# The first norm's shift and scale in three parts, and three tiles of q begun on two feature tiles

## The chip, the cores and the metric

The kernel runs on one core of one Trainium2 chip. A core has five engines that work beside each other, each through its own list of instructions in order: TensorE (PE in the profile, with its weight loads as PEld), VectorE (DVE), ScalarE (ACT), GpSimd (POOL) and SyncE (SP), which here only issues transfers. Transfers between the chip's memory and the core's own memory run on 16 DMA engines that all issuers share. Results of TensorE land in eight PSUM banks, from which DVE and ACT read.

The metric is the time of one execution on the device in microseconds. The three runs shown of the kernel before took 1045.0, 1046.94 and 1053.59 us, median 1046.94. The profile is one more execution, which took 1044.21 us.

## The reference, cut to what matters

One layer of a decoder is computed for 512 prompt tokens and 8 sample tokens, 520 columns in all, with 1024 features. The part that the change touches is its beginning:

```python
sh1, sc1, g1, sh2, sc2, g2 = split(silu(c) @ ada_w + ada_b, 6)     # c: 1 prompt row, 8 sample rows
h = rms_norm(x, norm1_g) * (1.0 + sc1) + sh1
z = h @ w_in        # columns: rg_x | rg_gate | q | k | v | forget | gateA | gateB
# branch A: conv, RG-LRU, gelu gate;  branch B: attention over q, k, v and paged caches
x = x + g1 * ((sigmoid(gA) * A + sigmoid(gB) * B) @ w_o)
x = x + g2 * SwiGLU(rms_norm(x) * (1.0 + sc2) + sh2)
```

All arrays are float32. `ada_w` is 1024 x 6144, so shift and scale of the first norm, its first 2048 columns, are 8.4 MB. The q columns of `w_in` are 1024 x 1024, 4.2 MB.

## The kernel before, in words

**Tiling.** Features lie on the 128 partitions, so x, the normed h and each result are eight feature tiles of 128 x 520. A product is computed in two halves of 260 columns (`HALVES`), one PSUM bank each. The matmuls run in a rounded float32 form; to keep the precision, every weight tile and every activation tile is split into a high part (`hi`, cast by ACT) and a low part (`lo`, the rest, by DVE), and each product of a 128 x 128 weight block is three matmuls: hi x hi, lo x hi, hi x lo (`q_matmuls`, L498 to L504). In the profile they carry the names whi, wlo (weights) and hh, hl (the normed activations).

**The start.** SP issues the loads in the order of the code: parameters, constants, the eight tiles of x, the page table twice (`ptb`, `idx`), then the weights. ACT squares x, DVE adds the squares, TensorE sums them over partitions (L509 to L519). `first_mod(fh, acc, kqs)` loads 128 rows of `ada_w`, 512 columns of the shift and 512 of the scale (512 KB), and multiplies them with silu(c): four narrow matmuls of 256 columns per row block, one for each quarter of the PE columns (profile name adaf). With `fh = 0` all eight row blocks come first. `first_mod_end` then brings the sums back: ACT copies them (adas), TensorE transposes them (adaft), DVE adds the bias (mod) and forms the amplitude (n1amp). That gives shift and scale of feature tiles 0 to 3. Meanwhile DVE computes 1/rms (L525) and scales x (xn, L528).

**h and the first six tiles of q.** `first_h(f)` makes one feature tile of h: ACT the high part of the 512 prompt columns, POOL the 8 sample columns (hr, L476 and L477), ACT their cast (L479), DVE the value (L478) and the low part (L480). The first six 128-column tiles of q are begun with feature tiles 0 to 3 alone, in two groups of three tiles (L538 to L551); the sums so far are kept in `qpart`. Within the first group the eight row blocks of `first_mod(1, ...)` are taken in between, one after every nine matmuls. `first_mod_end(1, ...)` and the h of feature tiles 4 to 7 stand after a quarter of the second group, so 54 matmuls of that group follow them. Later a second part of each q tile (`q_matmuls(1, ...)`) adds feature tiles 4 to 7 and DVE joins both (L878).

**What sets the order.** The code is recorded by a framework that orders each engine's instructions by its own estimates and places the waits; each engine then works strictly in that order. Buffers come from pools: 7 of 4 KB per partition for `ada_w` blocks and cache pages (tag pg), 2 for raw weights (tag wraw, which also holds the forget values of the cache, `past_load`, L405 to L407, gathered by an indirect transfer that POOL issues), 3 each for split weights (whi, wlo), 8 PSUM banks. An instruction that takes a buffer waits until its last reader is done. SP's transfers use eight completion counters in turn, so each transfer waits for the eighth before it.

Of the kernel before, what the change touches and what calls it, by code (L numbers as in the profile page):

```python
# [8 lines left out]
F32 = mybir.dt.float32  # L9
# [12 lines left out]
H = 16  # L22
# [42 lines left out]
def kernel(ctx, tc, xT, par, gates, b_f, cst, cse, own, cache_k, cache_v, cache_lf, pt,  # L65
# [377 lines left out]
    qpart = [slot("qp") for _ in range(6)]  # L443
    amp1 = keep.tile([128, KT, 9], F32, name="n1amp")

    def first_mod(fh, acc, kqs):
        for kq in kqs:
            raw = pgp.tile([128, 2, 512], F32, name="araw", tag="pg")
            sp.dma_start(raw, ada_w[kq * 128:kq * 128 + 128, :2048].rearrange("p (v c) -> p v c", v=2)
                         [:, :, 512 * fh:512 * fh + 512])  # L450
            for g in range(4):
                pe.matmul(acc[32 * g:32 * g + 32, :256], lhsT=silc[:, kq],
                          rhs=raw[:, g // 2, 256 * (g % 2):256 * (g % 2) + 256],
                          start=kq == 0, stop=kq == KT - 1, tile_position=(0, 32 * g))

    def first_mod_end(fh, acc):
        sb = slot("adas", 256)
        act.copy(sb, acc[:, :256])
        tp = bank(f"adaft{fh}")
        for b in range(2):  # L460
            pe.transpose(tp[:, b * 128:b * 128 + 128], sb[:, b * 128:b * 128 + 128], ident)
        tv = tp[:, :256].rearrange("p (b g c) -> p b g c", b=2, g=4)
        fs = slice(4 * fh, 4 * fh + 4)
        for v in (1, 0):
            dve.tensor_tensor(
                mod[:, v, fs].rearrange("p (q b) c -> p b q c", b=2), tv[:, :, 2 * v:2 * v + 2, 0:9],
                prm[:, fs, P_AB + v:P_AB + v + 1].rearrange("p (q b) c -> p b q c", b=2).to_broadcast([128, 2, 2, 9]),
                ALU.add)
        dve.scalar_tensor_tensor(amp1[:, fs], mod[:, 1, fs], 1.0, prm[:, fs, P_N1:P_N1 + 1].to_broadcast([128, 4, 9]),
                                 ALU.add, ALU.mult)  # L470

    def first_h(f):
        t, hi, lo = slot("hr"), slot("hh", dt=F32R), slot("hl", dt=F32R)
# [8 lines left out]

    xn = []

    def q_weights(fh, raw, ko, i):
# [5 lines left out]
        for k in range(0, 4, 2 if (fh, i) == (0, 0) else 4):  # L491
            ks = slice(k, k + 2 if (fh, i) == (0, 0) else 4)
            state["act"] = act.copy(hi[:, ks], src[:, ks])
            state["last"] = dve.tensor_tensor(lo[:, ks], src[:, ks], hi[:, ks].bitcast(F32), ALU.subtract)
# [15 lines left out]
    for f in range(KT):  # L510
# [9 lines left out]
    acc = [bank(f"adaf{fh}") for fh in range(2)]  # L520
    first_mod(0, acc[0], range(KT))
    r1 = slot("r1")
    for j, (t0, t1) in enumerate(HALVES):
        act.activation(r1[:, t0:t1], ssq[j][:, :HALF], AF.Sqrt, bias=eps, scale=1.0 / D)
        dve.reciprocal(r1[:, t0:t1], r1[:, t0:t1])  # L525
    for f in range(KT):
        t = slot("xn")
        dve.tensor_tensor(t, x[f], r1, ALU.mult)  # L528
        xn.append(t)
    raw = wraw()  # L530
    q_weights(0, raw, 0, 0)
    first_mod_end(0, acc[0])
    for f in range(4):
        first_h(f)
    q_weights(0, raw, 4, 2)
    raw = wraw()
    q_weights(0, raw, 0, 4)
    for g3 in (0, 3):  # L538
        banks = [bank(f"qp{i}_{j}") for i in range(g3, g3 + 3) for j in range(2)]
        for k in range(4):  # L540
            for n in range(6):
                q_matmuls(0, g3 + n // 2, n % 2, k, banks[n])
                if g3 == 0 and n % 3 == 2:
                    first_mod(1, acc[1], (2 * k + n // 3,))
            if g3 and k == 0:
                first_mod_end(1, acc[1])
                for f in range(4, KT):
                    first_h(f)
        for n in range(6):
            t0, t1 = HALVES[n % 2]  # L550
            act.copy(qpart[g3 + n // 2][:, t0:t1], banks[n][:, :HALF])  # L551
        if g3 == 0:
            flr = slot("flr", KT * H).rearrange("p (k c) -> p k c", k=KT)
            sp.dma_start(flr, w_in[:, COL_FL:COL_FL + H].rearrange("(k p) c -> p k c", p=128))
    raw = wraw()
    q_weights(1, raw, 0, 0)
    q_weights(1, raw, 4, 2)
# [1149 lines left out]
```

## Time and profile before

| | us |
|---|---|
| median of three runs (1045.0 to 1053.59) | 1046.94 |
| the profiled execution | 1044.21 |
| its span in the profile | 1042.3 |
| PE busy | 998.9 (96% of the span) |
| DVE busy | 777.5 (75%) |
| ACT busy | 533.2 (51%) |
| POOL busy | 304.0 (29%) |
| moved by DMA | 206.97 MB, mean 199 GB/s |

The span is the time from the first to the last recorded instruction; 1.9 us of the execution lie around it. The 40 slices of the page are 26 us each. A row of the timeline is: start in us, duration in us, engine, line of the kernel, operation, tile written <- tiles read, sizes, how many merged into the row, and in brackets how long the engine had been idle before and what ended it. A row of a table of stretches is: stretch, its length, then for each engine its busy time and count, then the granted TensorE clock (1.00 is full), the DMA share and GB/s.

### The profile page before, as it was taken

To read this page: it belongs to the slowest core of one execution; us is meant where nothing else is said; L and a number is where in the kernel's file an instruction comes from. 1 tells how busy PE (TensorE), PEld (TensorE's weight loads), DVE (VectorE), ACT (ScalarE), POOL (GpSimd) and SP (SyncE) were. 2 spreads that over 40 slices of the span, in tenths; PEclk is the share of its full clock that TensorE was granted. 3 is DMA by queue.
4 is the path that set the end of the run, shared out by engine and by line. 5 is a ranking of instruction groups with operands and counts; after the bars stand their busy time and mean duration, and the time that the engine had idled before them with its cause. 6 is when DMAs were issued, how large, how long until landed. Compare 5 with 4: busy or idle time off the path is not lost.

```text
span 1042.3 us, 21246 instructions
## 1 busy us (share of the span) xinstructions
PE 998.9 (96%) x8054; PEld 925.8 (89%) x8054; DVE 777.5 (75%) x1370; ACT 533.2 (51%) x1072; POOL 304.0 (29%) x411
## 2 busy tenths in 40 slices
PE   4999999999999999999999999899999999999993
PEld 1888899999898988878888989899999999999993
DVE  5447999988989978886665546778589558869663
ACT  4523665857671467767793234555244324524451
POOL 0224411112133235654500003472224033223113
PEclk9999999999999999999999999999999999999997
DMA  9898987787889999996766863132343234143212
GB/s 326 295 306 289 300 281 216 262 253 270 263 253 309 321 326 284 303 274 213 263 230 209 282 226 82 41 82 75 100 111 83 91 111 121 54 128 102 75 52 83
DMA packets 165353, 206.97 MB, mean 199 GB/s; under 512 B 9842, under 2 KB 126082, under 8 KB 165186
## 3 DMA queue, kind: packets, MB, share of 16 engines
q1 hardware_dynamic: 148530, 152.52, 47.2%
q0 software_dynamic: 13040, 46.67, 13.5%
q10 hardware_dynamic: 3680, 6.42, 1.7%
q8 instruction: 63, 1.03, 0.4%
q14 instruction: 40, 0.33, 0.1%
HBM read 192.49 MB, written 13.09 MB: 197 GB/s over the span
## 4 chain that ended last, share of the span: by engine, by line
PE 70%; DVE 12%; DMA 7%; ACT 5%; issue 4%; POOL 1%; SPq 0%; POOLq 0%; DVEq 0%; ACTq 0%
PE fo L281 11%; PE fi_S L1578 7%; PE fi_A L1578 5%; PE pb L281 4%; PE gb L281 4%; PE fig L281 4%; PE fiu L281 4%; PE ga L281 3%; PE k L281 3%; PE wo L281 3%; PE v L281 3%; DVE wlo L228 2%; PE gr L281 2%; PE xr L281 2%; DMA wraw<-in_w_in_dram 2%
## 5 line engine op out<-in xcount | busy, mean ns | idle before, releaser
L226 ACT CAST whi<-wraw 128x1024 fp32r<-128x1024 f32 (+2 forms) x113 | 111.4, 987 | 186.1 <-PE fo L281 45.0
L228 DVE TENSOR_TENSOR wlo<-wraw,whi 128x1024 fp32r<-128x1024 f32 (+2 forms) x113 | 137.3, 1216 | 48.6 <-ACT whi L226 40.9
L281 PE MATMUL fo<-ach,whi 128*128 128x260 f32 x302 | 85.6, 283 | 0.0
L281 PE MATMUL fo<-ach,wlo 128*128 128x260 f32 x302 | 85.2, 282 | 0.0
L281 PE MATMUL fo<-acl,whi 128*128 128x260 f32 x302 | 85.0, 282 | 0.0
L658 POOL DMA_DIRECT2D pg<-in_cache_k_dram x74 | 39.4, 533 | 142.4 <-DVE S L707 70.5
L241 POOL TENSOR_TENSOR ws<-wraw 128x512 f32<-128x512 f32 x13 | 20.0, 1538 | 193.5 <-DMA wraw<-in_w_fi_dram 188.7
L706 DVE TENSOR_TENSOR pg<-pg,qb 128x1024 f32<-128x1024 f32 x48 | 58.0, 1227 | 2.4 <-DMA pg<-in_cache_k_dram 2.4
L707 DVE TENSOR_REDUCE S<-pg 128x16 f32<-128x1024 f32 x48 | 57.0, 1207 | 0.1
L281 PEld LDWEIGHTS fo<-ach,whi 128*128 128x128 f32 x302 | 56.8, 188 | 0.2
L281 PEld LDWEIGHTS fo<-ach,wlo 128*128 128x128 f32 x302 | 56.8, 188 | 0.0
L281 PEld LDWEIGHTS fo<-acl,whi 128*128 128x128 f32 x302 | 56.8, 188 | 0.0
L1191 POOL TENSOR_SCALAR p<-p,mu 128x128 f32<-128x128 f32 (+3 forms) x28 | 35.9, 1293 | 48.2 <-DVE mu L1187 31.6
L249 DVE TENSOR_TENSOR wb<-ws,wb 128x512 fp32r<-128x512 f32 x52 | 45.8, 891 | 4.2 <-ACT wb L248 4.1
L373 POOL TENSOR_TENSOR ss<-ss,sq 128x260 f32<-128x260 f32 x18 | 13.7, 761 | 111.3 <-PE ada L344 58.9
L248 ACT CAST wb<-ws 128x512 fp32r<-128x512 f32 x52 | 31.5, 619 | 26.2 <-PE fi_S L1578 8.6
L1185 ACT ACTIVATE p<-p,mu 128x128 f32<-128x128 f32 (+3 forms) x64 | 35.3, 552 | 15.8 <-DVE mu L1184 15.5
L248 ACT CAST wb<-wraw 128x512 fp32r<-128x512 f32 x39 | 23.9, 620 | 34.7 <-PE fo L281 18.1
L1396 DVE SCALAR_TENSOR_TENSOR x<-fo,mod,x 128x252 f32<-128x252 f32 x32 | 15.2, 477 | 32.4 <-PE fo L281 32.4
L1435 ACT CAST ach<-sw 128x260 fp32r<-128x260 f32 (+1 forms) x42 | 17.6, 419 | 41.5 <-DVE sw L1477 22.3
L281 PE MATMUL v<-hh,whi 128*128 128x260 f32 x128 | 37.3, 291 | 1.1 <-DVE pl L1205 1.1
L1578 PE MATMUL fi_S<-twh,wb 128*128 128x260 f32 x208 | 38.1, 282 | 0.0
(435 smaller groups left out, 4065.7 us busy)
## 6 DMA issues: line engine op xcount, KB each, us to landing
araw<-in_ada_w_dram SPq DMA_DIRECT2D x48, 512.0 KB, 6.2
wraw<-in_w_fi_dram SPq DMA_DIRECT2D x44, 512.0 KB, 5.2
pg<-in_cache_k_dram POOLq DMA_DIRECT2D x42, 512.0 KB, 6.2
pg<-in_cache_v_dram SPq DMA_DIRECT2D x42, 512.0 KB, 5.5
wraw<-in_w_in_dram SPq DMA_DIRECT2D x34, 512.0 KB, 7.7
wraw<-in_w_in_dram SPq DMA_DIRECT2D x11, 1024.0 KB, 10.3
pg<-in_cache_v_dram POOLq DMA_DIRECT2D x22, 512.0 KB, 6.4
pg<-in_cache_k_dram POOLq DMA_DIRECT2D x32, 256.0 KB, 5.7
```

The costliest lines, as they stand in the source:

```text
L226: state["act"] = act.copy(hi[:, :k1 - k0], src)
L228: state["last"] = dve.tensor_tensor(lo[:, :k1 - k0], src, hi[:, :k1 - k0].bitcast(F32), ALU.subtract)
L241: pool.tensor_tensor(s1, a21, a22, ALU.add)
L248: state["act"] = act.copy(t[:, :4], src)
L249: state["last"] = dve.tensor_tensor(t[:, 4:], src, t[:, :4].bitcast(F32), ALU.subtract)
L281: state["mm"] = pe.matmul(out[:, :HALF], lhsT=wt[k], rhs=at, start=k == 0 and m == 0, stop=k == nk - 1 and m == 2)
L658: done.append(eng.dma_start(pg, cache[bass.ds(r, 1), :, c0:c1].rearrange("a p c -> (a p) c")))
L706: dve.tensor_tensor(pg, pg, q, ALU.mult)
L707: last = dve.tensor_reduce(S[r // 2][:, c:c + H], pg.rearrange("p (h d) -> p h d", d=DH), AX.X, ALU.add)
L1185: act.activation(p[:, :n + 128], p[:, :n + 128], AF.Exp, bias=mu[:, 0:1], scale=-1.0, accum_out=mu[:, 1:2])
L1191: (pool.tensor_scalar(p, p, mu[:, 2:3], None, ALU.mult) if a and i + 1 < KT else act.activation(p, p, AF.Copy, scale=mu[:, 2:3]))
L1578: state["mm"] = pe.matmul(b, lhsT=wt[k], rhs=at, start=k == 0 and m == 0, stop=k == 3 and m == 2)
```

## The change

`ada_w`'s columns for the first norm come in three parts. Features 0 to 255 and 256 to 511 are "quarters": 256 columns of shift and 256 of scale, eight loads of 256 KB each, matmuls of 128 columns (`quarter_load`, `quarter_mod`). Features 512 to 1023 come as before, eight loads of 512 KB (`first_mod`). `first_mod_end` takes the first feature tile and a count, and forms the amplitude ahead of the shift. The loads of the page table move from the start to behind the second quarter.

The weights of q for the first half of the features come in four parts of 256 rows by 384 columns (`q_part`), not three of 512 rows by 256 columns. After the first quarter, feature tiles 0 and 1 of h are made in halves, in place of xn (`early_h`), and q tiles 0 to 2 begin with them; the second quarter's matmuls lie between these. Then feature tiles 2 and 3 follow, then q tiles 3 to 5 with all four tiles, the third part's matmuls between them, and only then `first_mod_end(4, 2, ...)` and h of feature tiles 4 to 7.

```diff
-    sp.dma_start(ptb, pt.rearrange("a b -> (a b)")[None, :])
-    sp.dma_start(idx, pt.rearrange("a (b c) -> (a b) c", c=1))
...
+    def quarter_load(q, kq):
+        if kq % 2 == 0:
+            quarters[q, kq // 2] = pgp.tile([128, 2, 2, 256], F32, name="qraw", tag="pg")
+        sp.dma_start(quarters[q, kq // 2][:, kq % 2],
+                     ada_w[kq * 128:kq * 128 + 128, :2048].rearrange("p (v c) -> p v c", v=2)
+                     [:, :, 256 * q:256 * q + 256])
+
+    def quarter_mod(q, acc, kqs):
+        for kq in kqs:
+            raw = quarters[q, kq // 2][:, kq % 2]
+            for g in range(4):
+                pe.matmul(acc[32 * g:32 * g + 32, :128], lhsT=silc[:, kq],
+                          rhs=raw[:, g // 2, 128 * (g % 2):128 * (g % 2) + 128],
+                          start=kq == 0, stop=kq == KT - 1, tile_position=(0, 32 * g))
...
+    def early_h():
+        for f in range(2):
+            h.append((slot("hh", dt=F32R), slot("hl", dt=F32R)))
+        for j, (t0, t1) in enumerate(HALVES):
+            e_ = min(t1, NP)
+            for f in range(2):
+                t, (hi, lo) = xn[f], h[f]
+                a_, b_ = amp1[:, f, 0:1], mod[:, 0, f, 0:1]
+                act.activation(hi[:, t0:e_], t[:, t0:e_], AF.Identity, scale=a_, bias=b_)
+                if j:
+                    pool.tensor_tensor(t[:, NP:], t[:, NP:], amp1[:, f, 1:9], ALU.mult)
+                    pool.tensor_tensor(t[:, NP:], t[:, NP:], mod[:, 0, f, 1:9], ALU.add)
+                    act.copy(hi[:, NP:], t[:, NP:])
+                dve.tensor_scalar(t[:, t0:e_], t[:, t0:e_], a_, b_, ALU.mult, ALU.add)
+                dve.tensor_tensor(lo[:, t0:t1], t[:, t0:t1], hi[:, t0:t1].bitcast(F32), ALU.subtract)
...
+    def q_part(raw, k0, i, step):
+        src = raw[:, k0:k0 + 2]
+        sp.dma_start(src, w_in[128 * k0:128 * k0 + 256, COL_Q + 128 * i:COL_Q + 128 * i + 384]
+                     .rearrange("(k p) c -> p k c", p=128))
...
-    first_mod(0, acc[0], range(KT))
+    for kq in range(6):
+        quarter_load(0, kq)
+    q_part(raw, 0, 0, 1)
+    for kq in range(6, KT):
+        quarter_load(0, kq)
+    quarter_mod(0, accs[0], range(KT))
+    for kq in range(KT):
+        quarter_load(1, kq)
     r1 = slot("r1")
+    xn.extend(slot("xn") for _ in range(KT))
     for j, (t0, t1) in enumerate(HALVES):
         act.activation(r1[:, t0:t1], ssq[j][:, :HALF], AF.Sqrt, bias=eps, scale=1.0 / D)
         dve.reciprocal(r1[:, t0:t1], r1[:, t0:t1])
...
+        for f in range(2):
+            dve.tensor_tensor(xn[f][:, t0:t1], x[f][:, t0:t1], r1[:, t0:t1], ALU.mult)
+    first_mod_end(0, 1, accs[0])
+    early_h()
+    for f in range(2, KT):
+        dve.tensor_tensor(xn[f], x[f], r1, ALU.mult)
+    q_part(raw, 2, 0, 2)
+    sp.dma_start(ptb, pt.rearrange("a b -> (a b)")[None, :])
+    sp.dma_start(idx, pt.rearrange("a (b c) -> (a b) c", c=1))
...
+    for (j, k), kqs in zip(((0, 0), (0, 1), (1, 0), (1, 1)), ((0, 1, 2), (3,), (4, 5), (6, 7))):
+        for i in range(3):
+            q_matmuls(0, i, j, k, banks[i, j])
+        quarter_mod(1, accs[1], kqs)
+    first_mod_end(2, 1, accs[1])
+    first_h(2)
+    first_h(3)
+    q_part(raw, 0, 3, 2)
+    q_part(raw, 2, 3, 2)
+    acc = bank("adaf2")
+    for k in (2, 3):
+        for j in range(2):
+            for i in range(3):
+                q_matmuls(0, i, j, k, banks[i, j])
...
+    for k in range(4):
+        for j in range(2):
+            for i in range(3, 6):
+                q_matmuls(0, i, j, k, banks[i, j])
+            if k < 3 or j == 0:
+                first_mod(acc, ((0, 1), (2,), (3,), (4,), (5,), (6,), (7,))[2 * k + j])
+    first_mod_end(4, 2, acc)
+    for f in range(4, KT):
         first_h(f)
```

More of the change, by code (lines that the diff above doesn't have):

```diff
@@ L464, in first_mod_end @@
         for v in (1, 0):
[L465 to L470, printed above, removed]
+            bias = prm[:, fs, P_AB + v:P_AB + v + 1]
@@ L483 @@
     xn = []
+    def q_part(raw, k0, i, step):
+        src = raw[:, k0:k0 + 2]
+        sp.dma_start(src, w_in[128 * k0:128 * k0 + 256, COL_Q + 128 * i:COL_Q + 128 * i + 384]
+                     .rearrange("(k p) c -> p k c", p=128))
+        hi = wp.tile([128, 2, 384], F32R, name="whi", tag="whi", bufs=3)
+        lo = wp.tile([128, 2, 384], F32R, name="wlo", tag="wlo", bufs=3)
+        for k in range(0, 2, step):
+            ks = slice(k, k + step)
+            state["act"] = act.copy(hi[:, ks], src[:, ks])
+            state["last"] = dve.tensor_tensor(lo[:, ks], src[:, ks], hi[:, ks].bitcast(F32), ALU.subtract)
+        for n in range(3):
+            cs_ = slice(128 * n, 128 * n + 128)
+            qw.setdefault((0, i + n), []).extend((hi[:, k, cs_], lo[:, k, cs_]) for k in range(2))
     def q_weights(fh, raw, ko, i):
@@ L490, in q_weights @@
         src = raw[:, ko:ko + 4]
[L491 to L494, printed above, removed]
+        state["act"] = act.copy(hi, src)
+        state["last"] = dve.tensor_tensor(lo, src, hi.bitcast(F32), ALU.subtract)
         for n in range(2):
```

69 lines of the change are left out of this document (31 added, 38 removed).

## The prediction

> **What bounds the kernel now.** I read the page first (span, busy shares), then a table of stretches, then the timeline of the first 60 us, then the order and waits of the changed kernel as built.
>
> ```profile
> span 1042.3 us, 21246 instructions
> PE   4999999999999999999999999899999999999993
> ```
> ```profile
> 20.00:25.43 5.43, 1.97 (x18) 0.60 (x18) 4.49 (x10) 2.23 (x4) 0.95 (x2) 0.78 1.08 356
> 25.43:29.10 3.67, 3.67 (x15) 3.43 (x15) 3.56 (x7) 3.48 (x6) 3.48 (x6) 0.50 1.05 384
> ...
> 51.40:58.00 6.60, 6.60 (x58) 6.58 (x57) 4.33 (x7) 2.30 (x6) 1.59 (x3) 1.00 0.61 193
> ...
> 100.00:110.00 10.00, 9.36 (x78) 9.13 (x77) 10.00 (x20) 4.75 (x10) 7.49 (x15) 1.00 1.03 353
> 110.00:120.00 10.00, 9.23 (x74) 8.81 (x73) 9.79 (x25) 5.35 (x10) 4.66 (x10) 1.00 0.77 230
> ```
>
> TensorE is busy in every slice but the first and the last, so a microsecond that it loses or wins early moves the end, unless a later wait of its own takes it up. Up to 25.43 it starves: the first product of q begins then, and from there it runs without a pause. The change works on this start and on what follows up to about 59 us.
>
> ```profile
> 1.79 4.04 SPq L99 DMA_DIRECT2D x<-in_xT_dram  x8
> ...
> 9.04 2.67 ACT L512 ACTIVATE sq<-x 128x520 f32<-128x520 f32 x4 [0.48 <-DMA x<-in_xT_dram]
> ...
> 14.53 3.41 DVE L525 RECIPROCAL r<-r 128x260 f32<-128x260 f32 x2 [1.84 <-ACT r L524]
> ...
> 17.98 4.97 DVE L528 TENSOR_TENSOR xn<-x,r 128x520 f32<-128x520 f32 x8
> ...
> 22.04 0.64 PE L452 MATMUL adaf<-araw,silc 128*32 128x256 f32 x8 [0.73 <-DMA araw<-in_ada_w_dram]
> ...
> 23.17 0.69 PE L461 MATMUL adaft<-cs,adas 128*128 128x128 f32 x2 [0.49 <-ACT adas L458]
> 23.52 1.14 ACT L493 CAST whi<-wraw 128x512 fp32r<-128x512 f32 x2 [0.41 <-DMA wraw<-in_w_in_dram]
> 23.89 0.29 DVE L465 TENSOR_TENSOR mod<-adaft,prm 128x36 f32<-128x36 f32 x2 [0.94 <-PE adaft L461]
> ...
> 24.24 1.29 DVE L494 TENSOR_TENSOR wlo<-wraw,whi 128x512 fp32r<-128x512 f32 x2
> ...
> 24.57 0.81 ACT L475 ACTIVATE hh<-xn,mod,n1amp 128x512 fp32r<-128x512 f32 x1
> ...
> 25.43 0.58 PE L503 MATMUL qp<-hh,whi 128*128 128x260 f32 x1 [1.57 <-ACT hh L475]
> ```
> ```profile
> 18.00:21.00 3.00, 1.58 (x24) 0.43 (x24) 3.00 (x5) 0.00 (x0) 0.00 (x0) 1.00 1.04 383
> 22.00:25.00 3.00, 1.33 (x10) 0.45 (x10) 2.06 (x7) 1.85 (x4) 0.58 (x1) 0.68 1.09 349
> ```
>
> The last square begins at 9.04 + 3 x 0.67 = 11.0, so x has landed by then. The eight 512 KB blocks (4.19 MB) take until 22.04, 381 GB/s, and 3.4 us pass from the last block to the first product: copy, transposes, shift and scale, h. DMA is full the whole time.
>
> **Step 1, the start: -3.4 us.** Before the first product now stand eight quarters (2.10 MB) and 0.39 MB of weights. Their runs of 1 KB arrive as the weights of q do in the stretch 22 to 25, at 349 GB/s, not at the 383 of the 2 KB runs. The weights stand seventh: 1.97 MB, landed at 11.0 + 5.6 = 16.65. The last quarter: 18.15. Now DVE's list decides. Behind the first reciprocal (1.7, to 16.2) stand the two low parts of the weights, which wait for ACT's casts of 384 (0.43 each): 17.15 to 18.15. Then two half xn (0.31 each), to 18.75; the second reciprocal, to 20.45; the scale (0.15), 20.6; two half xn, 21.2; amplitude and shift, 21.5. ACT's half hh (0.45) ends at 21.95, TensorE starts at 22.05. The transfers alone would have let it start a good half microsecond to one earlier. Bounds: the weights at 383 GB/s land 0.5 earlier (-3.9); landing 2 later gives -1.4. The Trainium skill (DMA: Bandwidth & Descriptors, Specifications) gives 512 B as the least transfer for line rate, by which 1 KB runs would cost nothing against 2 KB; the trace differs with 349 against 383 GB/s. By that rule of the Trainium skill step 1 would be -3.9.
>
> **Step 2, work that moves onto TensorE's path: +3.1 us.** In the kernel before, the first eight groups of adaf ran while TensorE starved, the other eight inside q. Now eight quarter groups run while it starves, and eight quarter groups and eight full ones inside q.
>
> ```profile
> 33.29 0.64 PE L452 MATMUL adaf<-araw,silc 128*32 128x256 f32 x8
> ...
> 34.80 0.28 PE L503 MATMUL qp<-hl,whi 128*128 128x260 f32 x1
> 34.92 0.28 PE L503 MATMUL qp<-hh,whi 128*128 128x260 f32 x1
> 35.14 0.64 PE L452 MATMUL adaf<-araw,silc 128*32 128x256 f32 x8
> ```
> ```profile
> 60.18 1.06 PE L344 MATMUL ada<-araw,silc 128*32 128x512 f32 x8
> ```
>
> A group and nine products take 35.14 - 33.29 = 1.85; products follow each other at 0.12, so a group costs 1.85 - 9 x 0.12 = 0.77. One of 512 columns lasts 1.06 against 0.64: 0.42 per 256 columns, so 0.21 for 128 and 0.35 for changing over. As built, the second quarter is entered five times: 8 x 0.21 + 5 x 0.35 = 3.4. The third part is entered seven times: 8 x 0.42 + 7 x 0.35 = 5.8 for the 8 x 0.77 = 6.2 of before. One transpose more is 0.1. Bounds: columns free, 1.4; each quarter group as dear as a full one, 5.8. The 144 products stay, and I leave the 15 slow ones at the start (clock 0.50) as they are.
>
> **Step 3, behind the second quarter: +0.8 us.** The transpose of feature tiles 2 and 3 stands right behind the quarter's last group on TensorE and waits for ACT's copy, which stands behind a weight cast that waits for a buffer freed by the products just before. That is 0.5. Eleven products of q tiles 3 and 4 (1.3 us) then cover most of the way to hh; 0.3 is left. Bounds: 0, and 2.6, the time from 22.04 + 0.64 = 22.68 to 25.43 of before, less the one transpose that is saved.
>
> **Step 4, before the second half of the features: +4.3 us.** In the kernel before, this is hidden: shift and scale of tiles 4 to 7 come with 54 products still to do.
>
> ```profile
> 44.52 0.38 PE L461 MATMUL adaft<-cs,adas 128*128 128x128 f32 x2
> ...
> 51.24 0.28 PE L503 MATMUL q<-hh,whi 128*128 128x260 f32 x1
> ...
> 54.23 0.28 PE L503 MATMUL q<-hh,wlo 128*128 128x260 f32 x1
> ```
> ```profile
> 45.28 1.22 DVE L494 TENSOR_TENSOR wlo<-wraw,whi 128x1024 fp32r<-128x1024 f32 x1
> 46.41 0.54 DVE L478 TENSOR_SCALAR hr<-xn,n1amp,mod 128x512 f32<-128x512 f32 x1
> 47.27 0.73 DVE L480 TENSOR_TENSOR hl<-hr,hh 128x520 fp32r<-128x520 f32 x1 [0.32 <-ACT hh L479]
> ...
> 51.09 0.70 DVE L480 TENSOR_TENSOR hl<-hr,hh 128x520 fp32r<-128x520 f32 x1
> ```
> ```profile
> 45.40 0.82 ACT L475 ACTIVATE hh<-xn,mod,n1amp 128x512 fp32r<-128x512 f32 x1 [0.86 <-DVE n1amp L469]
> ...
> 50.03 1.05 ACT L493 CAST whi<-wraw 128x1024 fp32r<-128x1024 f32 x1 [0.38 <-ACT hh L479]
> ```
> ```profile
> 55.26 1.20 POOL L407 DMA_INDIRECT lfp<-in_cache_lf_dram,idx  x1 [5.93 <-DVE wlo L494]
> ```
>
> Now only nine products stand between the third part's last group and the two transposes. Call their end E. From transpose to amplitude pass 0.88 (44.52 to 45.40). On ACT a cast of 1.05 is queued ahead of the first hh, and its buffer comes free at E: hh of tile 4 runs from E + 1.1 to E + 1.9. On DVE follow the value of tile 4 (0.54, to E + 1.4), the low part of those weights (1.13 to the next), to E + 2.5, and four low parts with their values, 47.27 to 51.79 in the kernel before, 4.5: E + 7.0. The built order puts 25 products before the first one that needs the last low part, 54.23 - 51.24 = 3.0, and the transposes are 0.25: 3.8 of standing still. POOL adds 0.5: the gather lfp stands in its list before the shift of tile 5's sample columns, and its buffer waits for that same weight low part at E + 2.5; with 1.20 for itself and 0.4 for the shift the samples come at E + 4.1, ACT's cast is queued behind them, and DVE's low part of tile 5, else due at E + 3.8, at E + 4.3. Bounds: 3.3 (each low part 0.1 faster, no POOL delay) to 5.8.
>
> **Step 5, afterwards: -0.7 us.** TensorE's order is the same from there on. Of its 0.64 + 0.77 of waits from 100 to 120, when DVE is full, I take off half: one `ada_w` block and one gate block will have been loaded ahead of where TensorE is, so pages come a little earlier to DVE. Moving the page table costs nothing: POOL reads it between h of tiles 0 and 1 (to about 23) and that of tiles 2 and 3 (from 33); landing after 33, it would hold up that h by as much. SP issues nine transfers more, half a microsecond each (4.04 for eight of x); with eight in flight, over 2 MB, the full DMA covers them, and were it to run dry each would cost its 0.5 on step 1.
>
> **Sum:** -3.4 + 3.1 + 0.8 + 4.3 - 0.7 = +4.1, on the profiled 1044.2: 1048.3. The median of the runs lies 2.7 above the profiled execution, the lowest run 0.8; I add 1.2 and forecast **1049.5**, 0.4% slower. That is no change by what a measurement of this kernel can tell, about 1%. Its own range is 1047 to 1052.
>
> **Rival, faster: the delay is taken up later.**
>
> ```profile
> 200.00:300.00 100.00, 98.16 (x804) 90.95 (x803) 90.58 (x114) 70.19 (x124) 17.93 (x34) 1.00 0.80 256
> 300.00:400.00 100.00, 97.20 (x778) 88.34 (x780) 89.71 (x142) 46.35 (x99) 38.14 (x57) 1.00 1.00 306
> 400.00:500.00 100.00, 98.30 (x745) 83.09 (x738) 79.33 (x172) 74.49 (x187) 52.24 (x77) 1.00 0.87 263
> ```
>
> TensorE waits 1.8 + 2.8 + 1.7 = 6.3 here and 1.4 before. If these waits hang on the stream of cache pages through a full DMA to a 90% busy DVE, and that stream starts no later, all 7.7 can go: 4.8 - 7.7 = -2.9, 1042.5. It decides once more than 4.8 of them go. For it speaks the full DMA, against it that DVE and ACT are fed by TensorE's own results too. Chance 0.15.
>
> **Rival, the clock falls again.** The mean of 0.68 from 22 to 25 is 1.00 for 1.1 us and 0.50 after, so it fell at 23.1, although TensorE had been busy 1.58 of 3 us from 18 to 21. In step 4 it is busy 3.2 of 7.0. At 0.50 the 15 products from 25.43 took 3.67 in place of 1.8; as long a spell adds 2 to 3.4: 1051.5 to 1053. Chance 0.2. The Trainium skill (TensorE: Matmul & The Clock Gate, What's actually happening) lets it fall after an idle window of some 3.4 us; no pause here reaches 2 us, so by that rule the clock would hold and nothing be added; the trace speaks against it, since it fell at 23.1 without such a pause.
>
> **Rival, the change doesn't start q earlier:** quarters and weights land so late that the first product stays near 25.4. Then step 1 is nothing and the time 1053. DMA that is full speaks against it; chance 0.07.
>
> **How the numbers follow.** Forecast 0.5, the rivals 0.15, 0.2 and 0.07, unlisted slips 0.08. The range is 1042.5 to 1056: down to the faster rival, up to the clock's fall with step 2 at its upper bound (+2.7). Faster by over 1% (10.5 us) needs more than step 1 and all waits together: 0.02. Slower by over 1% needs the clock, a late start and an upper bound at once: 0.07. Within: 0.91.
>
> **What would show it.** The first product near 22; between 22 and 32 adaf records in five bunches; an idle TensorE of 3 to 5 us in two or three pieces near 52 to 59, waited for ACT hh and DVE hl; POOL's lfp in the middle of the hr rows; the clock after 52; the 26th product of the second half near 59, not 54.23. The prediction is wrong if that idle time is under 2, if the quarter groups cost under 0.25 each, or if the waits from 100 to 500 shrink by more than 3.

## The result and the profile after

| | kernel before | changed kernel |
|---|---|---|
| median | 1047.24 us (8 runs, 1045.0 to 1053.59) | 1054.97 us (8 runs, 1051.01 to 1058.55) |
| profiled execution, span | 1044.21, 1042.3 | 1056.78, 1055.1 |
| first product of q | 25.43 | 22.01 |
| first ada group | 60.18 | 66.24 |

The changed kernel takes 1.0058 times as long (95% interval 1.0031 to 1.0085, that is 3.2 to 8.9 us). The medians differ by 7.7 us, the two profiled spans by 12.8. By the bound of 1% that is no change; by the interval it is slower.

The slices of the changed kernel's page: TensorE is as full as before.

```profile
PE   4999999999999999999999999999999999999993
```

The timeline of the changed kernel, in the order of the prediction's steps:

```profile
22.01 0.39 PE L549 MATMUL qp<-hh,whi 128*128 128x260 f32 x1 [2.94 <-ACT hh L498]
...
32.05 0.33 PE L475 MATMUL adaft<-cs,adas 128*128 128x128 f32 x1 [0.56 <-ACT adas L472]
...
51.62 0.38 PE L475 MATMUL adaft<-cs,adas 128*128 128x128 f32 x2
53.64 0.39 PE L549 MATMUL q<-hh,whi 128*128 128x260 f32 x1 [1.63 <-ACT hh L509]
...
54.86 0.39 PE L549 MATMUL q<-hl,whi 128*128 128x260 f32 x1 [0.47 <-DVE hl L514]
...
56.40 0.49 PE L549 MATMUL q<-hh,whi 128*128 128x260 f32 x1 [0.80 <-ACT hh L513]
...
66.24 1.06 PE L344 MATMUL ada<-araw,silc 128*32 128x512 f32 x8
```
```profile
54.49 1.38 POOL L405 DMA_INDIRECT lfp<-in_cache_lf_dram,idx  x1 [0.24 <-DVE wlo L540]
55.90 0.22 POOL L511 TENSOR_TENSOR hr<-hr,mod 128x8 f32<-128x8 f32 x1
```
```profile
56.38 0.73 DVE L514 TENSOR_TENSOR hl<-hr,hh 128x520 fp32r<-128x520 f32 x1 [1.12 <-ACT hh L513]
...
58.93 0.70 DVE L514 TENSOR_TENSOR hl<-hr,hh 128x520 fp32r<-128x520 f32 x1
```

q starts 3.4 earlier, and at 51.62 the third part ends. From there TensorE stands still three times (1.63, 0.47, 0.80), and the first ada group, which stands at the same place in TensorE's list in both kernels, comes 66.24 - 60.18 = 6.06 later. From that point on TensorE's two lists are the same, so the lag can be read at any later product: 5.85 at 100 us of the kernel before, 7.31 at 130, 7.2 at 280, 8.8 at 300, 12.9 at 390, 12.8 at 1000. The lists of the other engines are not the same: the framework ordered them anew.

The table of stretches of the changed kernel shows what came on top of the 6.06:

```profile
53.11:56.52 3.41, 1.61 (x9) 1.20 (x10) 2.29 (x4) 1.65 (x5) 3.06 (x6) 1.00 1.05 406
56.52:59.94 3.42, 3.37 (x15) 3.07 (x16) 2.91 (x5) 3.09 (x10) 1.03 (x3) 0.50 1.11 374
105.00:130.00 25.00, 22.62 (x180) 21.57 (x179) 20.48 (x50) 11.85 (x24) 10.49 (x22) 1.00 0.86 274
285.22:288.63 3.41, 1.54 (x16) 1.05 (x9) 3.41 (x5) 3.38 (x7) 1.58 (x3) 1.00 0.43 115
288.63:292.04 3.41, 3.41 (x18) 3.41 (x17) 3.41 (x6) 2.04 (x7) 1.06 (x2) 0.50 1.02 345
391.03:394.44 3.41, 1.76 (x9) 1.29 (x10) 3.38 (x6) 2.94 (x6) 0.00 (x0) 1.00 1.03 393
394.44:397.86 3.42, 3.42 (x17) 3.42 (x18) 2.25 (x11) 1.96 (x9) 0.00 (x0) 0.50 1.05 331
```

TensorE waits 25 - 22.62 = 2.4 us between 105 and 130; over the same products, from 99 to 124, it had waited 1.4. And three times the granted clock is 0.50 for 3.41 us, called a half clock from here on: at 56.52, 288.63 and 394.44. At 288.63 the kernel before has the same wait of the same length, and no half clock:

```profile
280.34 0.51 PE L955 MATMUL gate<-xch,gws 128*128 128x260 f32 x2 [1.84 <-ACT gate L956]
```
```profile
275.66:279.08 3.42, 2.85 (x24) 1.79 (x22) 3.42 (x5) 2.35 (x4) 0.28 (x1) 1.00 0.60 169
279.08:282.49 3.41, 2.15 (x17) 2.15 (x18) 3.41 (x5) 3.40 (x9) 1.83 (x4) 1.00 0.68 240
```

All starts of a half clock in one execution lie whole multiples of 3.413 us apart. In the changed kernel the 1.87 us of that wait fell into one such interval (busy 1.54 of 3.41), in the kernel before it was cut by a boundary (2.85 and 2.15).

Of the 6.8 us that the lag grows behind the ada group, 1.2 come by 130 us, 1.5 with the half clock at 288.63, and 4.1 between 300 and 390. They come with the half clock at 394.44 and, ahead of it, with waits for DVE and ACT that sum to 2.3 us, where the first profile of the kernel before has 0.75 and its second (c0 below) 2.0.

### The profile page after: what moved, and what is told of

It is laid out like the page before. It is cut to its first block, busy times and chain, and to the rows that moved or that the text cites. A ratio compares the mean times of both kernels' runs of the same rounds, so it can differ in the third digit from the quotient of the medians.

```text
span 1055.1 us, 21395 instructions
## 1 busy us (share of the span) xinstructions
PE 1007.3 (95%) x8118; PEld 933.1 (88%) x8118; DVE 780.7 (74%) x1380; ACT 533.6 (51%) x1076; POOL 299.9 (28%) x411
## 4 chain that ended last, share of the span: by engine, by line
PE 75%; DVE 12%; DMA 4%; ACT 4%; issue 2%; POOL 1%; SPq 0%; POOLq 0%; ACTq 0%; DVEq 0%
PE fo L281 11%; PE fi_S L1647 7%; PE fi_A L1647 5%; PE pb L281 4%; PE gb L281 4%; PE fiu L281 4%; PE v L281 4%; PE fig L281 4%; PE k L281 4%; PE pa L281 3%; PE wo L281 3%; PE ga L281 3%; PE gr L281 2%; PE pv L860 2%; DMA wraw<-in_w_in_dram 2%
## 5 line engine op out<-in xcount | busy, mean ns | idle before, releaser
L241 POOL TENSOR_TENSOR ws<-wraw 128x512 f32<-128x512 f32 x13 | 17.5, 1345 | 194.5 <-DMA wraw<-in_w_fi_dram 186.5
L1647 PE MATMUL fi_A<-h2h,wb 128*128 128x260 f32 x208 | 38.2, 284 | 0.0
```

The source lines that it names most:

```text
L1647: state["mm"] = pe.matmul(b, lhsT=wt[k], rhs=at, start=k == 0 and m == 0, stop=k == 3 and m == 2)
```

## Experiments: what holds TensorE between 51 and 66 us

**The third part earlier (e1_cover).** Four of the eight row blocks go into the first group of q tiles, so that some 40 products follow the last block, not 9.

```diff
     for k in (2, 3):
         for j in range(2):
             ...
+            first_mod(acc, (2 * k + j - 4,))
...
-            if k < 3 or j == 0:
-                first_mod(acc, ((0, 1), (2,), (3,), (4,), (5,), (6,), (7,))[2 * k + j])
-    first_mod_end(4, 2, acc)
-    for f in range(4, KT):
-        first_h(f)
+            if 2 * k + j < 3:
+                first_mod(acc, ((4, 5), (6,), (7,))[2 * k + j])
+            if 2 * k + j == 2:
+                first_mod_end(4, 2, acc)
+                for f in range(4, KT):
+                    first_h(f)
```

> The changed kernel with the third part's groups begun ten products earlier: four row blocks inside the first group of q tiles, four in the second, so that about 40 products stand behind the last block in place of 9. Theory (the chain from the third part's last block to the last low part of tile 7, 8.0 us in the changed kernel, stands open): 40 products of 0.12 and the 25 that need no last low part cover 7.8 of 8.0; TensorE's waits for hh and hl before the second half of the features fall from 2.9 us to under 0.7, no half clock near 57, the first ada group stands near 60.8 and not at 66.24, and the median falls by 5 us, to about 1050. Rival 1 (the third part's loads are late, because its eighth block waits for the buffer of its first): TensorE waits for araw instead, 2 us or more, and the time is 1053 or above. Rival 2 (what is won early is lost again at 100 to 500): the ada group near 61, but the median above 1053.

Measured: 1054.76 us (1.0064, 1.004 to 1.0089), the ada group at 65.98. The theory fell, and so did both rivals: TensorE didn't wait for araw, and nothing was won at the ada group that could be lost later. ACT's, POOL's and TensorE's timelines of this run say why:

```profile
53.25 1.05 ACT L539 CAST whi<-wraw 128x1024 fp32r<-128x1024 f32 x1 [1.57 <-issue]
...
57.52 0.20 ACT L513 CAST hh<-hr 128x8 fp32r<-128x8 f32 x1 [1.70 <-POOL hr L511]
```
```profile
55.87 1.37 POOL L405 DMA_INDIRECT lfp<-in_cache_lf_dram,idx  x1 [2.26 <-DVE wlo L540]
```
```profile
48.10 0.42 PE L475 MATMUL adaft<-cs,adas 128*128 128x128 f32 x2
...
57.77 0.39 PE L549 MATMUL q<-hh,whi 128*128 128x260 f32 x1 [0.79 <-ACT hh L513]
```

The transposes came 3.5 earlier, and the h of tiles 6 and 7 didn't follow: ACT's third weight cast stood 1.57 us, with hh of those tiles queued behind it, and POOL's gather waited for the low part of those weights, with the samples of tile 7 behind it.

**The two queues cleared (e9_queue).** The same, with POOL's gather put behind the samples of tile 7 (`hr` is POOL's last instruction for them) and the third weight cast behind ACT's last hh:

```diff
-            past_load()
+            with tc.issue_after(state["hr"].ins):
+                past_load()
...
-    q_weights(1, raw, 0, 4)
+    with tc.issue_after(state["hh"].ins):
+        q_weights(1, raw, 0, 4)
```

> The run with the earlier third part, and beside it two queues cleared: POOL's gather lfp behind the samples of tile 7, and ACT's third weight cast (with its low part on DVE) behind the last hh; that cast had stood 1.57 us at 53.25 for a buffer, with hh of tiles 6 and 7 behind it. Theory (the end of the third part was covered, but the h of tiles 4 to 7 stood behind a cast that waits for the last products of the first half, and behind the gather): TensorE's waits at 54 to 58 (0.47, 0.41, 0.79) all go, no half clock near 58, the first ada group 0.4 to 1.0 us later than the 60.18 of the kernel before, and few waits at 100 to 130: median 1048 to 1049.5. Rival (the casts and the gather only swap places with other waits, for the weights' low part held back): the group above 63 and the median above 1052.

Measured: the waits of 0.47, 0.41 and 0.79 are gone but for 0.29, the clock holds there, and the ada group stands at 62.00, 4.2 earlier than in the changed kernel (0.8 later than expected). So the two queues together were what held it; this run doesn't say what each is worth. The median, 1053.48 (1.0061, 1.0039 to 1.0082), missed the expectation by 4; the section on what becomes of a delay takes that up.

**The gather alone (e2_gather)** has the first hunk of that diff and nothing else.

> The changed kernel with POOL's gather lfp held back until the sample columns of tile 7 are shifted. Theory (the gather holds up tile 5's samples and so the whole row of low parts): the shift of tile 5 ends near 54.5 and not 56.12, the wait of 0.80 for hh ahead of tile 5 is gone, tile 7's low part ends near 58.7 and not 59.63, and the first ada group stands 0.5 to 0.9 earlier than 66.24: median 1054.3. Rival (the half clock from 56.5 on sets the pace there, not the low parts): the group stands less than 0.3 earlier where the clock has fallen, and more than 1.2 earlier where it has not.

Measured: 1053.36 us (1.0066, 1.0041 to 1.0091), and in the timeline and the stretches:

```profile
52.02 0.38 PE L475 MATMUL adaft<-cs,adas 128*128 128x128 f32 x2
...
57.78 0.38 PE L549 MATMUL q<-hl,whi 128*128 128x260 f32 x1 [0.28 <-DVE hl L514]
...
65.09 1.06 PE L344 MATMUL ada<-araw,silc 128*32 128x512 f32 x8
```
```profile
58.29 0.70 DVE L514 TENSOR_TENSOR hl<-hr,hh 128x520 fp32r<-128x520 f32 x1
```
```profile
53.57:56.98 3.41, 2.19 (x13) 1.78 (x14) 3.25 (x5) 2.56 (x7) 3.25 (x5) 1.00 1.05 409
56.98:60.40 3.42, 3.14 (x25) 2.81 (x24) 2.62 (x5) 2.35 (x8) 2.03 (x4) 1.00 0.28 89
```

Counted from the transposes, the last low part ends after 6.97 us in place of 8.01, and the ada group comes after 13.07 in place of 14.62. Of those 1.55, the earlier low parts are 1.0. The other 0.5 is put down to the half clock, which this run doesn't have there: the 26th product of the second half starts at 59.04, 0.05 behind the last low part, and in the changed kernel at 60.30, 0.67 behind it. That price is low because the low parts set the end of this stretch in any case. The group stands 1.15 earlier than 66.24, more than the theory's 0.5 to 0.9 and just under the rival's 1.2; low parts and clock each have a share.

**The wait filled (e3_fill)**: 13 products behind the transposes (`tp` is the last of them), into a bank that is free.

```diff
     first_mod_end(4, 2, acc)
+    with tc.issue_after(state["tp"].ins):
+        for n in range(13):
+            pe.matmul(acc[:, :HALF], lhsT=h[0][0][:, :128], rhs=h[0][0][:, :HALF], start=True, stop=True)
```

> The changed kernel with 13 more products, whose result nobody reads, behind the transposes of the third part, in the wait of 1.63 us for hh of tile 4: TensorE is busy there. Theory (the clock falls after an interval of 3.4 us in which TensorE is busy less than half, and the last low part at 59.63 sets the end of this stage in any case): no half clock between 50 and 62, and still the first ada group only 0.5 us earlier, near 65.7; median lower by 0.5, 1054.5. Rival (the price that the prediction set, 2 to 3.4 us for the clock): the group near 63 to 64 and the median near 1052.

```profile
53.50:56.91 3.41, 2.05 (x13) 1.44 (x11) 2.29 (x4) 1.66 (x5) 3.06 (x6) 1.00 1.06 408
56.91:60.33 3.42, 3.26 (x15) 2.95 (x15) 2.79 (x5) 2.96 (x10) 0.90 (x2) 0.50 1.09 366
```

Measured: 1053.53 us (1.0068, 1.0043 to 1.0094), the ada group at 66.57, 14.68 behind the transposes as in the changed kernel (14.62). The first wait was filled, and the clock fell all the same. Theory and rival both had the group earlier, and it isn't. The run says little about the first wait, though: in this execution the interval ahead of the fall begins at 53.50, when the filled wait was nearly over. The two later waits were enough, with TensorE recorded busy for 2.05 of 3.41.

## Experiments: what the start is worth

**The second reciprocal later (e5_recip; `amp` is the first amplitude), the page table at the start again (e4_tables), the second quarter in one bunch (e6_bunch).**

```diff
-        dve.reciprocal(r1[:, t0:t1], r1[:, t0:t1])
+    for j, (t0, t1) in enumerate(HALVES):
+        with tc.issue_after(state["amp"].ins) if j else nullcontext():
+            dve.reciprocal(r1[:, t0:t1], r1[:, t0:t1])
         for f in range(2):
             ...
-    first_mod_end(0, 1, accs[0])
+        if j == 0:
+            first_mod_end(0, 1, accs[0])
```
```diff
     ptb = keep.tile([1, NS * NPAGE], I32, name="ptb")
     idx = keep.tile([NS * NPAGE, 1], I32, name="idx")
+    sp.dma_start(ptb, pt.rearrange("a b -> (a b)")[None, :])
+    sp.dma_start(idx, pt.rearrange("a (b c) -> (a b) c", c=1))
...
     q_part(raw, 2, 0, 2)
-    sp.dma_start(ptb, pt.rearrange("a b -> (a b)")[None, :])
-    sp.dma_start(idx, pt.rearrange("a (b c) -> (a b) c", c=1))
```
```diff
-    for (j, k), kqs in zip(((0, 0), (0, 1), (1, 0), (1, 1)), ((0, 1, 2), (3,), (4, 5), (6, 7))):
+    for (j, k), kqs in zip(((0, 0), (0, 1), (1, 0), (1, 1)), ((), (), (), range(KT))):
```

> The changed kernel with DVE's second reciprocal behind the first amplitude. Theory (step 1: DVE's list, not the transfers, decides when q starts): the first product at 20.3 to 21.0 in place of 22.01. Rival (the last quarter's landing decides): 21.8 or later. At 51.6, where the third part ends, the theory leaves 0.3 to 1.0 of it, since the second halves come later by the same reciprocal; the median falls by that much, below what the runs can tell.

> The changed kernel with the two loads of the page table at the start again, behind x. Theory (their move costs and brings nothing, since DMA is full there): the first product of q within 0.3 of 22.01, the first ada group within 0.4 of 66.24, the median within 2 of 1055. Rival (two issues of 0.5 us on SP ahead of all weights count): the first product 0.6 to 1.0 later, and the median about 1056.

> The changed kernel with all eight groups of the second quarter in one bunch behind the first 36 products, not in five. Theory (step 2: each change between products and groups costs 0.35 us): four changes less, the third part's transposes at 50.2 to 50.6 in place of 51.62. Rival (some groups filled pauses in which TensorE waited for low parts, so that they cost less than they seemed): less than 0.5 earlier.

| run | first product | transposes | half clock from the first product on | median |
|---|---|---|---|---|
| changed kernel | 22.01 | 51.62 | 3.41 us (22.39 to 25.80) | 1054.97 |
| e5_recip | 20.52 | 51.25 | 5.99 (to 26.51) | 1058.85 (1.0086, 1.0053 to 1.012) |
| e4_tables | 20.79 | 51.58 | 6.12 (to 26.91) | 1055.07 (1.0086, 1.0059 to 1.0113) |
| e6_bunch | 21.74 | 50.60 | 5.48 (to 27.22) | 1055.61 (1.0078, 1.0052 to 1.0103) |

DVE's list does decide when q starts: with the reciprocal out of the way it starts at 20.52. With the page table back at the start it also came 1.2 earlier, which neither theory nor rival had. DVE of the changed kernel and of e4 shows that it is the same reciprocal: the framework's order changed with the edit, and both reciprocals stand ahead of the low parts of the weights.

```profile
18.57 1.77 DVE L580 RECIPROCAL r<-r 128x260 f32<-128x260 f32 x1
```
```profile
14.15 3.42 DVE L582 RECIPROCAL r<-r 128x260 f32<-128x260 f32 x2 [1.84 <-ACT r L581]
```

Yet little of these 1.2 to 1.5 us is left at the transposes: 0.04 in e4, 0.37 in e5. The stretches of the run with the reciprocal show where it went:

```profile
19.68:23.09 3.41, 2.57 (x26) 2.28 (x30) 3.41 (x8) 1.57 (x3) 0.84 (x2) 0.50 1.10 350
23.09:26.51 3.42, 3.42 (x40) 2.33 (x33) 3.33 (x9) 1.74 (x5) 0.55 (x3) 0.50 1.07 366
```

q started inside the half clock and ran 2.6 us longer at it; products there follow at 0.22 us in place of 0.12, so about 1.2 is lost. How long the half clock lasts differs from execution to execution too: e1 starts q at 22.31 and runs 5.3 us at it. The median of e5 rose by 3.9 where a fall was expected; its profiled execution has five half clocks behind 30 us. The bunch won 1.0 at the transposes; with 0.27 from its earlier start taken off and about 1.0 for its longer half clock put back, the four changes come to some 1.7, against 4 x 0.35. It lost that in a half clock of 6.83 us from 54.53 on.

## Experiments: what becomes of a delay

**A delay alone (e7_delay)**: the kernel before with 48 products between the two halves of q.

```diff
+    for n in range(48):
+        pe.matmul(acc[1][:, :HALF], lhsT=h[0][0][:, :128], rhs=h[0][0][:, :HALF], start=True, stop=True)
     raw = wraw()
     q_weights(1, raw, 0, 0)
```

> The kernel before with 48 more products, whose result nobody reads, between the first and the second half of the features of q: TensorE is held up by 48 x 0.12 = 5.8 us without standing still, about as much as the changed kernel is late at 60 us. Theory (a delay at 60 us goes through to the end, and the waits from 100 to 130 grow from the delay alone): +5.8 and 0 to 1.2 more, 1053 to 1054.3. Rival 1 (the faster rival of the prediction: later waits take the delay up): less than +4, at most 1051. Rival 2 (the waits from 100 to 130 grow through the changed order of the loads, not through the delay): +5.8 with the waits from 100 to 130 at 1.4 as before.

Measured: 1057.29 us (1.0084, 1.0058 to 1.011), 9.7 above before for 5.7 of delay, and above the theory's range. The lag on the kernel before is 5.2 at 60 us, 5.0 at 100, 7.9 at 130 and 11.6 at 300. Rival 1 falls: nothing is taken up. Of the 2.9 by which the lag grows from 100 to 130, 1.6 are longer waits (28 - 25.01 = 3.0 us for 1.4) and the rest is the half clock that begins at 120.92:

```profile
104.00:132.00 28.00, 25.01 (x192) 24.36 (x191) 24.86 (x56) 14.60 (x30) 11.02 (x22) 0.94 0.82 252
```
```profile
120.34 0.50 PE L957 MATMUL gate<-xch,gws 128*128 128x260 f32 x2 [2.43 <-ACT xch L314]
```

Rival 2 isn't settled by this run. TensorE's products keep their order, but the framework ordered the other engines anew: DVE of the kernel before (first) takes two page products and then their sums, in e7 (second) a sum stands behind each product, as in the changed kernel.

```profile
101.31 1.21 DVE L702 TENSOR_TENSOR pg<-pg,qb 128x1024 f32<-128x1024 f32 x1
...
102.52 1.22 DVE L702 TENSOR_TENSOR pg<-pg,qb 128x1024 f32<-128x1024 f32 x1
...
103.75 1.21 DVE L703 TENSOR_REDUCE S<-pg 128x16 f32<-128x1024 f32 x1
```
```profile
101.90 1.45 DVE L704 TENSOR_TENSOR pg<-pg,qb 128x1024 f32<-128x1024 f32 x1
...
104.40 1.20 DVE L705 TENSOR_REDUCE S<-pg 128x16 f32<-128x1024 f32 x1
```

Four profiles with one order of all engines from 66 to 128 us and a lag of 5.9 to 6.3 at 100 show how far these waits differ by themselves: the changed kernel above, and in this order e3, e4 and e6.

```profile
105.00:130.00 25.00, 23.65 (x193) 23.00 (x192) 22.57 (x54) 13.08 (x27) 13.06 (x25) 1.00 0.83 272
```
```profile
105.00:130.00 25.00, 24.13 (x198) 23.64 (x197) 22.27 (x52) 13.62 (x28) 12.24 (x24) 1.00 0.86 278
```
```profile
105.00:130.00 25.00, 23.59 (x193) 22.95 (x192) 22.16 (x51) 13.28 (x27) 11.48 (x19) 1.00 0.83 267
```

TensorE waits 2.4, 1.4, 0.9 and 1.4 us, for 1.4 before. So longer waits there are not shown to follow from the delay.

**A lead (e10_all, e15_turn, e14_best).** e10 is e9 with the reciprocal and the bunch of the section above; e15 puts the first work on the gathered forget values one q tile later; e14 takes the third part by twos as well (second hunk).

```diff
-            past_turn(0)
         if i == 7:
+            past_turn(0)
             past_turn(1)
```
```diff
-            first_mod(acc, (2 * k + j - 4,))
+            if j:
+                first_mod(acc, (2 * k - 4, 2 * k - 3))
...
-            if 2 * k + j < 3:
-                first_mod(acc, ((4, 5), (6,), (7,))[2 * k + j])
+            if 2 * k + j in (0, 2):
+                first_mod(acc, ((4, 5), (), (6, 7))[2 * k + j])
```

> The same, and beside it the second reciprocal behind the first amplitude, and the second quarter in one bunch. Theory: q starts 1 us earlier than 22.01 and the second quarter costs up to 1.4 less, so that the first ada group stands at 58.3 to 59.5, ahead of the 60.18 of the kernel before, and the median is 1045 to 1047, at or below the kernel before (1047.3). Rival (a lead at 60 us is lost in the waits from 100 to 500, which hang on loads that do not come earlier): the group ahead of 60.18, the median at 1047.5 to 1050.

> The run with everything (third part early, queues cleared, reciprocal behind, second quarter in one bunch), and beside it the first half of the work on the gathered forget values one q tile later, so that POOL issues the load of the second q row (at 94.27 there, 88.31 in the kernel before) ahead of it. That run stood level with the kernel before at 100 us and then waited 3.4 us for a weight's low part at 110, behind page products that came late. Theory (the page stream held up on POOL makes that wait): the wait at 110 falls below 1, the position at 130 us is level with the kernel before within 1, and the median 1047 to 1049. Rival (DVE's built order has the low part behind the page sums in any case): the wait stays at 3 and the median at 1051 to 1052.

> The same with the third part's eight groups taken by twos, four changes less of 0.35: the first ada group 1.0 to 1.4 earlier than in that run, at about 59, ahead of the 60.18 of the kernel before; if the lead goes through, the median is 1046 to 1047, 0 to 0.2% below the kernel before. Rival (the lead is lost in the waits from 100 to 130): 1047.5 to 1049, no faster than the kernel before.

Measured: e10 stands at 60.43 at the ada group (58.3 to 59.5 expected) and level with the kernel before at 100 us (100.05 for 100.01), and then waits: 3.35 at 110, with a half clock from 110.22 on. It takes 1051.78 us (1.0029, 1.0009 to 1.005), above what theory and rival had. e9 does the same, with 3.26. POOL and TensorE of e10, and DVE of e9:

```profile
94.27 0.54 POOL L750 DMA_DIRECT2D qb<-qtd  x1
```
```profile
110.39 0.58 PE L281 MATMUL ga<-hh,wlo 128*128 128x260 f32 x1 [3.35 <-DVE wlo L228]
```
```profile
105.83 1.49 DVE L774 TENSOR_TENSOR pg<-pg,qb 128x1024 f32<-128x1024 f32 x1 [1.92 <-DMA pg<-in_cache_k_dram]
...
110.37 1.21 DVE L228 TENSOR_TENSOR wlo<-wraw,whi 128x1024 fp32r<-128x1024 f32 x1
```

In the kernel before that load of a q row stands at 88.31. Behind it come the cache pages, and DVE takes two pages and their sums ahead of the low part for which TensorE waits. With POOL's list put right (e15) that wait is 0.57, as the theory had it; but another of 1.85 opens at 116, at 130 us it is 2.9 behind and not level, and the median is 1050.82 (1.0035, 1.0018 to 1.0052). e14 has its lead, 59.54 for 60.18, but only 0.3 on e15's 59.84: as built, its third part is entered six times for seven, since the framework took the pairs apart again, and one change less at 0.35 is what that is worth. It has the same new wait as e15:

```profile
116.17 0.39 PE L1032 MATMUL gate<-xcl,gws 128*128 128x260 f32 x1 [1.85 <-DVE xcl L315]
```
```profile
110.00:120.00 10.00, 8.03 (x65) 7.61 (x64) 9.96 (x20) 4.53 (x8) 5.45 (x10) 1.00 0.65 193
```

It takes 1052.69 us (1.0041, 1.0021 to 1.0061), above theory and rival; its interval and e15's overlap. None of these versions beats the kernel before: DVE is busy for 9.96 of the 10 us from 110 to 120, and in each of them a wait opens there. Which order of pages, weights and sums would avoid them stays open.

**The kernel before once more (c0_before)**, unchanged.

> The kernel before, unchanged, profiled once more. Theory (the profiled execution of before, 1044.2, was one without a half clock between 29.9 and 1030, while most executions have one to three such intervals of 3.4 us behind waits that all of them share, and that is why the median of the kernel before lies 3 above its profiled execution): this execution shows at least one half clock between 30 and 1030, each worth 1.5 to 1.7, and waits of the same length as in the first profile; span 1043.5 to 1048. Rival (the executions differ by their waits, not by the clock): no half clock there, and a span above 1044 through longer waits.

```profile
664.57 0.68 PE L380 MATMUL r<-ss,cs 128*128 128x260 f32 x2 [2.23 <-DVE ss L373]
```
```profile
661.97:665.38 3.41, 1.18 (x9) 0.94 (x8) 1.49 (x5) 2.09 (x4) 0.00 (x0) 1.00 0.75 215
665.38:668.80 3.42, 3.42 (x18) 3.42 (x18) 0.00 (x0) 2.04 (x3) 0.00 (x0) 0.50 0.40 97
```

Measured: 1047.27 us, span 1045.3, 3.0 above the first profile: one half clock at 665.38 worth 1.5 (behind a wait of 2.23 that the first execution has with 2.22 and no fall), 0.6 by a longer wait near 107, and the rest, about 1, between 300 and 500. So both were true in part. Half clocks between 30 and 1030 in all profiles:

| | ada group | lag at 130 us | half clocks begin at | median - before |
|---|---|---|---|---|
| before, c0 | 60.18, 60.34 | 0, 0.6 | none; 665 | 0 |
| changed kernel | 66.24 | 7.3 | 57, 289, 394 | 7.7 |
| e1 | 65.98 | 6.9 | 58, 393 | 7.2 |
| e2 | 65.09 | 5.1 | 286, 671 | 5.8 |
| e3 | 66.57 | 6.1 | 57, 391 | 6.0 |
| e4 | 66.68 | 5.5 | 58, 286, 672 | 7.6 |
| e5 | 66.32 | 9.0 | 57, 122, 289, 395, 678 | 11.0 |
| e6 | 66.30 | 5.9 | 55 (6.83 long), 287, 392 | 7.8 |
| e7 | 65.36 | 7.9 | 121, 292, 677 | 9.7 |
| e9 | 62.00 | 4.4 | 112, 286 | 5.7 |
| e10 | 60.43 | 3.0 | 110, 284, 670 | 4.0 |
| e15 | 59.84 | 2.9 | 116, 389 | 3.3 |
| e14 | 59.54 | 1.5 | 283, 389 | 5.2 |

The last column is the lag at 130 us and 0 to 2 more (-0.1 to 2.1) in all rows but that of e14. The half clocks near 285 and 670 stand behind waits that every kernel has (1.8 to 1.9 us, in e7 2.7, and 2.1 to 2.2), and come in some profiles and not in others. Near 392 the waits differ themselves, from 0.75 to 2.5 us, and the half clock comes only in profiles with 1.4 or more.

## Why the prediction was right or wrong

The class (no change by 1%) and the range (1042.5 to 1056) held; the forecast of 1049.5 was 5.5 too low, and the forecast's own range of 1047 to 1052 was missed. That the wide range held is in part luck: its upper end was set by a fall of the clock at 2 to 3.4 us and step 2 at its bound, and other terms carried the time there.

1. **Step 1, -3.4: right in size and cause.** 22.01 for a forecast of 22.05, and DVE's list decides (e5, e4). The runs of the weights are 1.5 KB (384 columns) and not 1 KB as the step says; they are 0.39 MB of 2.5. What the step didn't say: this start lies in a half clock, so an earlier one is mostly lost again. The changed kernel kept its lead because it ran only 3.41 us of q at half clock, for 4.47 before.
2. **Steps 2 and 3, +3.1 and +0.8: right.** From the first product to the end of the transposes behind the first half (0.25) it takes 51.87 - 22.01 = 29.86, before 51.24 - 25.43 = 25.81: +4.05 for 3.9, the shorter half clock helping by about 0.5. The wait ahead of the transpose is 0.56 for 0.5; the 0.3 behind it didn't come.
3. **Step 4, +4.3: right mechanism, term too small.** From the end of the transposes, E, to the ada group 14.37, before (from 51.24) 8.94: +5.4, near the upper bound of 5.8. Without the gather it is 12.82, +3.9 for the 3.8 of the step (e2). The gather delays the last low part by 1.0 and not 0.5, and the half clock costs about 0.5 that the step had left to a rival. TensorE's recorded waits come to 2.9, for the 3 to 5 named; from start to start of the products they are 1.91 + 0.76 + 1.08 less 3 x 0.12, 3.4, since a record lasts 0.28 and products follow at 0.12. One reason given was incomplete: that the kernel before hides this through its 54 products. Some 40 products behind the third part hid next to nothing (e1) until the cast and the gather no longer stood in the queue (e9).
4. **Step 5, -0.7: not borne out, its sign open.** The lag grows by 1.2 from 60 to 130 us in this execution. In e3, e4 and e6, with the same order of all engines from 66 to 128 us and a lag of 6.1 to 6.5 at 60, it shrinks by 0.3, 1.0 and 0.3. So neither half the waits, as the step had it, nor longer ones are shown to come with a later TensorE; what decides between 0.9 and 2.4 us of them stays open.
5. **From the profiled execution to the median, +1.2: too small.** The profiled execution of before had no half clock between 29.9 and 1030; the medians of the kernel before beside the experiments, 1047.5 to 1047.8, lie 3.3 to 3.6 above it, and c0 shows of what kind these are. 1044.2 + 7.3 (lag at 130) + 3.3 is 1054.8, for a measured median of 1054.97. The closeness is in part chance, since the lag at 130 is that of one execution, and the same sum misses most other runs by up to 2 us and e14 by 3.7.
6. **The rivals.** "The delay is taken up later" fell: e7 took nothing up, and in the changed kernel the waits over the products from 200 to 500 are 7.0 us for 6.3. "The clock falls again" came true at 56.52, at 0.5 and not at 2 to 3.4, because the low parts set the end there (e2); it fell twice more in this execution, at 288.63 and 394.44, at about 1.5 each. "q doesn't start earlier" fell with 22.01. By the rule cited from the Trainium skill (TensorE: Matmul & The Clock Gate, What's actually happening), an idle window of some 3.4 us is needed; the trace disagrees, since in the window ahead of the fall at 56.52 TensorE was idle for 1.8 of 3.41 us.

Summed up, in the profiled execution and the medians: steps 1 to 4 missed 1.3, step 5 1.9, the way to the median 2.1 to 2.4. The interval of 3.2 to 8.9 us on the measured difference is wide beside the last two.

## What to carry to other kernels

Cover is counted in what the queue can reach, not in products: before trusting it, look at what stands ahead of the needed instruction on each engine and which buffer that one waits for. An inserted delay isn't a clean test where a framework orders the engines by its own estimates: compare the other engines' lists before reading a wait as its effect. Before adding to one profiled time, see which half clocks that execution had, and how far the waits differ between profiles of one order.

## What the hardware showed that was not expected

The clock falls on a raster of 3.41 us whose position differs from one execution to the next. The same wait near 285 (1.8 to 1.9 us, in e7 2.68) stands ahead of a half clock in nine of fourteen profiles, and in the five of before, c0, e1, e3 and e15 it does not; one half clock is worth 1.5 to 1.7 us where TensorE is full. The Trainium skill (TensorE: Matmul & The Clock Gate, What's actually happening) says of this window that it is free-running and doesn't start with the kernel; the trace agrees: in two executions of the kernel before the boundaries lie at 23.08 and 29.90, and at 23.68 and 30.50.

An interval needn't be idle for the clock to fall. Over the fourteen profiles, from the first half clock to 1030 us, all 16 intervals at full clock with TensorE recorded busy for at most 1.57 of 3.41 us were followed by one at 0.50, of the 28 with 1.58 to 2.06 18 were, and of the others, with 2.08 or more, none. The interval with 2.05 lost the clock (53.50 in e3), but this one of the kernel before with 1.74 kept it, so the recorded share alone doesn't decide it:

```profile
661.37:664.78 3.41, 1.74 (x13) 1.71 (x14) 0.95 (x4) 2.72 (x4) 0.00 (x0) 1.00 1.05 286
```

Back to full takes more: the intervals at 0.50 with 2.77 or less were followed by another at 0.50, those with 2.91 or more by one at 1.00. The one in e6 that made its half clock 6.83 us long:

```profile
54.53:57.94 3.41, 2.62 (x11) 2.32 (x11) 2.39 (x5) 2.83 (x10) 1.86 (x6) 0.50 1.02 401
```
